# Pairs of weight blocks in the split products of w_in: four products with the high parts, then two with the low parts

## The chip, the cores and the metric

The kernel runs on one core of one Trainium2 chip. The metric is the device time of one execution in microseconds (us). The engines go by the names of the profile: PE is TensorE (its matrix products), PEld its loads of weights, DVE is VectorE, ACT is ScalarE, POOL is GpSimd, and SP is the queue that issues most DMAs.

## The reference

One layer over 512 latent and 128 context tokens (640 in all), all in float32, cut here to what comes before, in and behind the changed products:

```python
D_MODEL = 2048
P_IN = C_SHIFT + 2 * D_B          # 3360 + 2048 columns

def _layer(x, mod, s0, shift_fn, lp):
    sh1, sc1, g1, sh2, sc2, g2 = jnp.split(mod, 6, axis=-1)
    h = _rmsnorm(x, lp['norm1_g']) * (1.0 + sc1) + sh1
    p = h @ lp['w_in']
    o_a, s_fin = _rwkv7_bidir(shift_fn(p[..., :C_SHIFT], lp['mu_shift']), s0, lp)
    o_b = _chunk_gmlp(jax.nn.gelu(p[..., C_SHIFT:]), lp)
    x = x + g1 * (jnp.concatenate([o_a, o_b], axis=-1) @ lp['w_out'])
    h = _rmsnorm(x, lp['norm2_g']) * (1.0 + sc2) + sh2
    ff = (jax.nn.silu(h @ lp['w_ffn_gate']) * (h @ lp['w_ffn_up'])) @ lp['w_ffn_down']
    return x + g2 * ff, s_fin
```

The change is in `p = h @ lp['w_in']` alone. `_rwkv7_bidir` is a two-way recurrence over 16 heads, which the kernel works off in chunks of 64 tokens; `_chunk_gmlp` mixes tokens within chunks of 128.

## The kernel before

**Stages.** The w_in stage (with the modulation and the normalisation ahead of it), the recurrence together with w_out, and the feed-forward part. They share PE, one after the other.

**The w_in stage.** `h` lies transposed in SBUF, 16 blocks of 128 rows by 640 tokens, split into two float32r tiles: `h_hi` and `h_lo`, the rest that the rounding left. `w_in` comes in 43 column blocks of 128, each in four pieces of 512 rows (256 KB). `split` loads a piece (L167, issued from SP), casts it to `hi` on ACT (L168) and takes the rest `lo` on DVE (L169), with three buffers for each of the three tiles; `prefetch` runs two pieces ahead. `win` works off one piece: for each half of the tokens (320 columns) and each of its four blocks it issues three products of 128x128 weights by 320 columns, hi by h_hi (L190), hi by h_lo (L191) and lo by h_hi (L192). They add up in one PSUM tile `big` per half over the four pieces of a block, 48 products in all; the last one closes the sum. Over the stage there are 4128 of these wide products.

**What lies between them.** When a block is done, `take` copies it to SBUF (`praw`, ACT L959) and hands it to a generator that works it off in small steps: the token shift, per pair of heads (eight pairs, two directions each) the key normalisation (products `pmm`, L519), decay and gate (`pwa`, L592 and L593, read by ACT as sg and tha, L596), the Gram matrices of the chunks (`pG`, L651, copied as GB, L655 and L663), transposes (`pXT`, L669, copied as XT, L675, and stored to DRAM, L677) and a product `pW` (L683, copied as Z, L685), and for the gMLP blocks a gelu (`gq`, L706 to L713). `pmm`, `pwa`, `pG`, `pXT` and `pW` share two PSUM tiles, so each waits until its forerunner there has been copied out; XT has two SBUF buffers. A second generator, `solve`, takes the Gram blocks through DRAM (`mix<-dd`, by POOL's queue) and inverts them on DVE (from L802 on); a third, `merge`, fetches the result (`TB<-d`, POOL's queue) and puts it together by five small products per direction (`pblk` L843, `pM` L868 copied as `M` L871, `pT` L877 copied as TF, L880). Beside these, four more columns of modulation weights are loaded (1 MB each, L893) and multiplied (`pm`, L906).

**What sets the order.** Behind the second and the fourth block of a half (`GRAN`), `between` lets each of the three queues of generators run for a budget of estimated costs. The generators thus hand their instructions out at fixed places of the program; but outside the first part of the stage and the recurrence, the order on each engine is that of the scheduler, which works through the program by its dependences. Each engine takes its instructions strictly in that order.

## Time and profile before

| | us |
|---|---|
| median of 3 timed runs | 3223.48 (3221.9 to 3225.47) |
| the profiled execution | 3213.3 |
| its span, first to last instruction | 3211.5 |
| mean granted clock of PE | 0.991 |
| first and last start of L190 | 49.4 and 1078.8 |

A row of a group of instructions reads: line, engine, operation, tile written <- tiles read, shapes, count, then busy time and the mean ns of one, then the idle time of the engine just before them and what ended it. Products overlap in PE's pipeline, so 0.31 us of busy time each does not say how far apart they start; the timeline's start column does. An idle time in brackets is one in which no product was under way. The line numbers in the profile are those of the kernel before.

### The profile page before, as it was taken

Reading aid. Unit: us, or ns where it says so; the run is one execution under the profiler, and the core shown is the slowest. Engines: PE = TensorE matmul, PEld = TensorE weight load, DVE = VectorE, ACT = ScalarE, POOL = GpSimd, SP = SyncE. Lnnn points to the kernel's source line nnn. Section 1 sums busy time; section 2 is a strip of 40 time slices with the busy share of each in tenths; the row PEclk is TensorE's granted clock in tenths of the full one; section 3 lists DMA queues with packets and bytes.
Section 4 is the critical chain, followed back from the end, with each engine's and each line's share of the span. In section 5 each row is a group of like instructions: output and inputs, shape, how many; then the busy total and the mean of one; then the engine's idle time right before and its main releaser. Section 6 shows DMA issues by size and latency. Waiting matters only on the chain.

```text
span 3211.5 us, 72260 instructions
## 1 busy us (share of the span) xinstructions
PE 3088.0 (96%) x28216; PEld 2858.2 (89%) x28216; DVE 2330.3 (73%) x4107; ACT 1460.1 (45%) x3197; POOL 1219.0 (38%) x1065
## 2 busy tenths in 40 slices
PE   6999989999999999999999999999999999999997
PEld 3688778788878888899999999999999999999997
DVE  4558666676657677767877777777777788887788
ACT  3344544454444444346644444444444454444365
POOL 2001121211122024311465566556655645555542
PEclk9999999999999999999999999999999999999999
DMA  9767786777778687564434434343344364553453
GB/s 372 239 187 203 210 215 171 209 218 193 201 198 216 210 275 253 173 200 133 141 116 130 127 105 123 118 124 118 113 128 126 104 199 152 159 165 112 140 165 122
DMA packets 740438, 550.88 MB, mean 172 GB/s; under 512 B 141056, under 2 KB 673504, under 8 KB 731264
## 3 DMA queue, kind: packets, MB, share of 16 engines
q1 hardware_dynamic: 727136, 532.47, 55.0%
q0 software_dynamic: 10624, 13.23, 1.9%
q8 instruction: 222, 3.64, 0.5%
q14 instruction: 120, 0.98, 0.1%
q10 hardware_dynamic: 2336, 0.57, 0.1%
HBM read 437.79 MB, written 110.95 MB: 171 GB/s over the span
## 4 chain that ended last, share of the span: by engine, by line
PE 56%; DVE 5%; issue 4%; DMA 3%; POOL 2%; ACT 2%; SPq 0%; DVEq 0%; POOLq 0%; ACTq 0%
PE P L1644 15%; PE P L1642 15%; PE P L1643 15%; DVE lo L1424 1%; PE big L1482 1%; PE big L1484 1%; PE big L1483 1%; PE big L1039 1%; PE big L190 1%; PE big L192 1%; PE big L191 1%; PE big L1041 1%; PE big L1040 1%; DMA opd<-d_op 1%; DMA rawd<-in_w_ffn_down_dram 1%
## 5 line engine op out<-in xcount | busy, mean ns | idle before, releaser
L1644 PE MATMUL P<-xo,lo 128*128 128x320 f32 x2352 | 727.1, 309 | 0.8 <-DVE lo L1424 0.7
L1642 PE MATMUL P<-xo,hi 128*128 128x320 f32 x2352 | 727.0, 309 | 0.7 <-ACT hi L1423 0.7
L1643 PE MATMUL P<-xo,hi 128*128 128x320 f32 x2352 | 726.9, 309 | 0.0
L1424 DVE TENSOR_TENSOR lo<-raw,hi 128x512 fp32r<-128x512 f32 x526 | 500.8, 955 | 174.4 <-ACT hi L1423 169.9
L1423 ACT CAST hi<-raw 128x512 fp32r<-128x512 f32 x526 | 326.7, 621 | 484.0 <-PE P L1643 392.1
L190 PE MATMUL big<-h_hi,hi 128*128 128x320 f32 x1376 | 447.3, 325 | 8.1 <-ACT hi L168 4.5
L1644 PEld LDWEIGHTS P<-xo,lo 128*128 128x128 f32 x2352 | 441.5, 188 | 1.8 <-DVE lo L1424 1.8
L1642 PEld LDWEIGHTS P<-xo,hi 128*128 128x128 f32 x2352 | 441.6, 188 | 1.0 <-ACT hi L1423 1.0
L1643 PEld LDWEIGHTS P<-xo,hi 128*128 128x128 f32 x2352 | 441.6, 188 | 0.0
L192 PE MATMUL big<-h_hi,lo 128*128 128x320 f32 x1376 | 431.1, 314 | 0.7 <-DVE lo L169 0.6
L191 PE MATMUL big<-h_lo,hi 128*128 128x320 f32 x1376 | 431.1, 313 | 0.7 <-DVE h_lo L352 0.4
L1552 POOL TENSOR_TENSOR raw<-raw 128x512 f32<-128x512 f32 x252 | 408.5, 1631 | 14.1 <-DVE lo L1424 2.7
L1644 PE MATMUL P<-xd,lo 128*128 128x320 f32 x1232 | 384.5, 312 | 16.3 <-DVE lo L1424 16.2
L1642 PE MATMUL P<-xd,hi 128*128 128x320 f32 x1232 | 382.7, 311 | 1.5 <-ACT hi L1423 0.3
L1643 PE MATMUL P<-xd,hi 128*128 128x320 f32 x1232 | 381.4, 310 | 0.0
L169 DVE TENSOR_TENSOR lo<-raw,hi 128x512 fp32r<-128x512 f32 x268 | 183.4, 689 | 200.6 <-ACT hi L168 185.1
L190 PEld LDWEIGHTS big<-h_hi,hi 128*128 128x128 f32 x1376 | 260.9, 190 | 58.1 <-issue 34.8
L1423 ACT CAST hi<-rawd 128x512 fp32r<-128x512 f32 (+1 forms) x288 | 168.8, 587 | 240.7 <-PE P L1643 203.1
L168 ACT CAST hi<-raw 128x512 fp32r<-128x512 f32 x268 | 164.5, 618 | 225.7 <-PE big L191 123.8
L191 PEld LDWEIGHTS big<-h_lo,hi 128*128 128x128 f32 x1376 | 261.3, 190 | 5.1 <-DVE h_lo L352 1.1
L192 PEld LDWEIGHTS big<-h_hi,lo 128*128 128x128 f32 x1376 | 260.3, 189 | 5.6 <-DVE lo L169 1.6
L1644 PEld LDWEIGHTS P<-xd,lo 128*128 128x128 f32 x1232 | 231.9, 188 | 23.2 <-DVE lo L1424 22.8
(404 smaller groups left out, 6052.8 us busy)
## 6 DMA issues: line engine op xcount, KB each, us to landing
wt<-in_w_mod_dram SPq DMA_DIRECT2D x96, 1024.0 KB
raw<-in_w_ffn_gate_dram SPq DMA_DIRECT2D x182, 256.0 KB
raw<-in_w_ffn_up_dram SPq DMA_DIRECT2D x182, 256.0 KB
rec<-d_S SPq DMA_DIRECT2D x80, 576.0 KB
raw<-in_w_in_dram SPq DMA_DIRECT2D x172, 256.0 KB
rawd<-in_w_ffn_down_dram SPq DMA_DIRECT2D x128, 256.0 KB
raw<-in_w_out_dram SPq DMA_DIRECT2D x96, 256.0 KB
xd<-d_os SPq DMA_DIRECT2D x66, 320.0 KB
```

What stands on the lines that cost most here:

```text
L168: S.copy(hi, raw)
L169: V.tensor_sub(lo, raw, hi.bitcast(F32))
L190: TE.matmul(halves[hf], hi[:, k, :], h_hi[:, kb, s], start=(kb == 0), stop=False)
L191: TE.matmul(halves[hf], hi[:, k, :], h_lo[:, kb, s], start=False, stop=False)
L192: TE.matmul(halves[hf], lo[:, k, :], h_hi[:, kb, s], start=False, stop=(kb == KB - 1))
L1039: TE.matmul(halves[hf], hi[:, k, :], o_hi[kb][:, s], start=(k == 0), stop=False)
L1423: S.copy(hi[:, 0:nk], raw[:, 0:nk])
L1424: V.tensor_sub(lo[:, 0:nk], raw[:, 0:nk], hi[:, 0:nk].bitcast(F32))
L1552: G.tensor_tensor(out=o[:, 0:nk], in0=p[:, 0:nk], in1=q[:, 0:nk], op=ALU.subtract)
L1642: TE.matmul(ps, hi[:, k, :], xk[:, 0, :], start=f, stop=False)
L1643: TE.matmul(ps, hi[:, k, :], xk[:, 1, :], start=False, stop=False)
L1644: TE.matmul(ps, lo[:, k, :], xk[:, 0, :], start=False, stop=l)
```

## The change

The core of the diff:

```diff
@@ -189,7 +189,9 @@
                 kb = 4 * q + k
                 TE.matmul(halves[hf], hi[:, k, :], h_hi[:, kb, s], start=(kb == 0), stop=False)
                 TE.matmul(halves[hf], hi[:, k, :], h_lo[:, kb, s], start=False, stop=False)
-                TE.matmul(halves[hf], lo[:, k, :], h_hi[:, kb, s], start=False, stop=(kb == KB - 1))
+                if k % 2:
+                    for j in (kb - 1, kb):
+                        TE.matmul(halves[hf], lo[:, j - 4 * q, :], h_hi[:, j, s], start=False, stop=(j == KB - 1))
                 wide[0] += 1
                 step(k)
```

The two lo products of blocks 0 and 1, and those of blocks 2 and 3, now stand together behind the four hi products of the same blocks. Number, shapes and operands of the products stay; the sum in PSUM gets its terms in another order. `step(k)` hands out small work at k = 1 and 3 only, so it still comes behind a whole pair. From L192 on, the changed kernel's line numbers are two higher (its lo products are L194).

The scheduler answers with another order of the small work on PE, ACT, DVE and SP between wide products 384 and 3974 of the stage, mostly by a few places. The first of the two places that matter is on PE, in the fifth pair of heads. Before, the merge of the fourth pair begins behind wide product 2328 (`pblk`):

```order
L192 MATMUL big<-h_hi,lo 128x320
L843 MATMUL pblk<-TB,A__1119 32x32 x2
L725 MATMUL pw<-ident,wsp 128x128
L843 MATMUL pblk<-TB,A__1119 32x32
L651 MATMUL pG<-R,X 128x128 x4
L190 MATMUL big<-h_hi,hi 128x320
```

and behind wide product 2376, with the transposes `pXT` 25 to 33 wide products back, comes

```order
L192 MATMUL big<-h_hi,lo 128x320
L906 MATMUL pm_6577<-wt,cT 2x512 x8
L843 MATMUL pblk<-TB,A__1119 32x32 x14
L683 MATMUL pW_7173<-Z,GA 64x64 x10
L843 MATMUL pblk<-TB,A__1119 32x32 x23
L592 MATMUL pwa<-wa,wh 128x320
```

Now nothing small stands behind product 2328; the merge begins behind 2352, and behind 2376 stands

```order
L194 MATMUL big<-h_hi,lo 128x320 x2
L908 MATMUL pm_6577<-wt,cT 2x512 x2
L671 MATMUL pXT<-ident,X 128x64 x16
L908 MATMUL pm_6577<-wt,cT 2x512 x2
L845 MATMUL pblk<-TB,A__1119 32x32 x4
L671 MATMUL pXT<-ident,X 128x64 x4
L908 MATMUL pm_6577<-wt,cT 2x512 x4
L685 MATMUL pW_7173<-Z,GA 64x64 x10
L594 MATMUL pwa<-wa,wh 128x320
```

The first part of the merge moved 24 wide products back, and the transposes (L669, now L671) moved behind product 2376, directly ahead of `pW` (L683, now L685).

The second place is on ACT, in the third pair of heads, where the second pair's `M` is copied. Before:

```order
L675 COPY XT<-pXT 128x128 x2
L685 COPY Z<-pW_4747 64x5x64 x2
L685 COPY Z<-pW_4748 64x5x64 x2
L711 ACTIVATE gq<-gq 128x640
L959 COPY praw<-big 128x320
L871 COPY M_5109<-pM_5143 32x320 x2
```

Now:

```order
L677 COPY XT<-pXT 128x128
L687 COPY Z<-pW_4747 64x5x64 x2
L677 COPY XT<-pXT 128x128
L713 ACTIVATE gq<-gq 128x640
L961 COPY praw<-big 128x320
L687 COPY Z<-pW_4748 64x5x64 x2
L873 COPY M_5109<-pM_5143 32x320 x2
```

The last two copies of Z moved behind the tanh of the gelu (L711, now L713). On PE the second `pmm` product (L519), which writes to the tile that these copies read, stands behind wide product 1720 now (1715 before), and `pT` behind 1728 as before. On DVE, in the same place, the gelu's product `gq` (L709) and the wait of `solve` for its DMA (L802) stood so before:

```order
L755 TENSOR_TENSOR vt_4929<-vt_4929,lng 128x640
L802 COPY mx_1121<-mix 80x2x15
L169 TENSOR_TENSOR lo<-raw,hi 128x512
L806 TENSOR_TENSOR mix<-mx_1121,mix 80x2x28
L756 TENSOR_TENSOR vt_4929<-vt_4929,lnb 128x640
L808 TENSOR_TENSOR mx_1121<-mx_1121,mix 80x2x14x2
L709 TENSOR_TENSOR gq<-gq,praw 128x640
```

and stand so now:

```order
L169 TENSOR_TENSOR lo<-raw,hi 128x512
L757 TENSOR_TENSOR vt_4929<-vt_4929,lng 128x640
L804 COPY mx_1121<-mix 80x2x15
L711 TENSOR_TENSOR gq<-gq,praw 128x640
L808 TENSOR_TENSOR mix<-mx_1121,mix 80x2x28
```

`gq` (now L711) comes directly behind L802 (now L804) instead of four instructions later.

## The prediction

> **What bounds the kernel now.** I read the page first, then the windows by stage, then the timeline of TensorE inside the w_in stage, then its waits. The page:

> ```profile
> span 3211.5 us, 72260 instructions
> PE 3088.0 (96%) x28216; PEld 2858.2 (89%) x28216; DVE 2330.3 (73%) x4107; ACT 1460.1 (45%) x3197; POOL 1219.0 (38%) x1065
> L190 PE MATMUL big<-h_hi,hi 128*128 128x320 f32 x1376 | 447.3, 325 | 8.1 <-ACT hi L168 4.5
> L192 PE MATMUL big<-h_hi,lo 128*128 128x320 f32 x1376 | 431.1, 314 | 0.7 <-DVE lo L169 0.6
> ```

> PE is busy 96% of the span and nearly nothing ends late before the three lines that the change reorders: 0.7 us of idle time before all 1376 products of L192. These lines run from 49 to 1079 us. The windows of that stage and of what follows (columns: length, then each engine's busy time and instructions, then the granted clock, DMA share and GB/s):

> ```profile
> 160.00:420.00 260.00, 254.68 (x2403) 216.66 (x2402) 171.81 (x331) 116.80 (x245) 36.80 (x61) 1.00 0.73 203
> 420.00:660.00 240.00, 225.47 (x2768) 186.43 (x2768) 154.00 (x310) 112.57 (x250) 43.33 (x73) 0.98 0.73 199
> 660.00:1080.00 420.00, 404.12 (x5474) 346.62 (x5474) 284.91 (x577) 200.28 (x429) 79.66 (x125) 1.00 0.72 197
> ```

> So PE is the stage's bound. Its open idle time is 5.3 + 14.5 + 15.9 = 35.7 us (length less busy); that is all a better order could take away. The order of the engines' instructions differs only up to the first instructions of the next stage, so I cost the w_in stage alone.

> **The products themselves: 0.** The same 4128 products are issued; what changes is which follows which. A piece of the timeline shows the pace and the price of an interruption by small products (start, busy, engine, line):

> ```profile
> 1070.10 0.31 PE L190 MATMUL big<-h_hi,hi 128*128 128x320 f32 x1
> 1070.24 0.31 PE L191 MATMUL big<-h_lo,hi 128*128 128x320 f32 x1
> 1070.39 0.31 PE L192 MATMUL big<-h_hi,lo 128*128 128x320 f32 x1
> 1070.54 0.31 PE L190 MATMUL big<-h_hi,hi 128*128 128x320 f32 x1
> 1070.68 0.31 PE L191 MATMUL big<-h_lo,hi 128*128 128x320 f32 x1
> 1070.83 0.31 PE L192 MATMUL big<-h_hi,lo 128*128 128x320 f32 x1
> 1071.07 0.82 PE L868 MATMUL pM<-TB,GB 32*32 32x32 f32 x40
> 1071.82 0.41 PE L190 MATMUL big<-h_hi,hi 128*128 128x320 f32 x1
> 1072.07 0.31 PE L191 MATMUL big<-h_lo,hi 128*128 128x320 f32 x1
> ```

> From 1070.10 to 1070.83 five steps take 0.73 us, 146 ns each. L190 to L191 keeps the weights and changes the moving tile; L191 to L192 changes both; L192 to L190 changes the weights and keeps h_hi's tile. All cost the same. The new order has only steps of these kinds (two lo products in a row change weights and moving columns), so it neither gains nor loses at the pace. The page's means (325 against 314) are not a price of the first product: they hold the longer one behind an interruption.

> **Fewer interruptions: -1.2 us.** Leaving the wide run costs 1071.07 - 1070.83 - 0.15 = 0.09 us, coming back 1072.07 - 1071.82 - 0.15 = 0.10: about 0.2 us for a round trip. Counted along PE's order there are 305 such trips before and 299 after: 6 x 0.2 = -1.2 us (bounds -1.2 and 0, if the small products then stand in worse places).

> **The later low part: -0.6 us.** A lo tile is now needed behind four products of its piece rather than two, 2 x 0.146 = 0.29 us later. What waits for it (us, times, before the load of weights of L192):

> ```profile
>   DVE lo L169: 2.2, 4
> ```

> Four waits can each lose at most 0.29 us: -1.2 us; they may go to another wait behind them: 0. I take the middle. No DMA and no queue is moved past by this itself: hi is needed as early as before, the last product of a block is still a lo product, so the copy of its result (L959) starts as before, and the hi buffer is free one product sooner for a cast (L168) that PE hardly waits for (4.5 us above).

> **The rearranged small work.** This is where time can come and go. PE's waits in the stage (total, times, longest):

> ```profile
> PE pT L877 <- ACT M L871: 4.6, 4, 3.4
> PE pW L683 <- ACT XT L675: 3.8, 4, 1.7
> PE pwa L592 <- ACT Z L685: 2.3, 3, 1.0
> ```

> Two places carry most of the difference; the order rows stand in the part on the change. The first is the merge of the fourth pair and the transposes of the fifth. Before, pblk (L843) came 24 wide products sooner than it now does and waited for its DMA:

> ```profile
> 630.48 0.22 PE L843 MATMUL pblk<-TB,A__1119 32*32 32x32 f32 x2 [1.24 <-DMA TB<-d]
> 631.51 0.22 PE L843 MATMUL pblk<-TB,A__1119 32*32 32x32 f32 x2 [0.55 <-DMA TB<-d]
> 645.32 0.42 PE L592 MATMUL pwa<-wa,wh 128*128 128x320 f32 x1 [0.42 <-ACT Z L685]
> ```

> 24 x 0.146 = 3.5 us covers that: -1.8 us. In exchange the transposes pXT (L669), which had 33 wide products between them and pW (L683), stand directly ahead of it with only ten small ones of L906 and L843. That is a figure that the kernel already has in two other places, of which the dearer reads:

> ```profile
> 427.12 0.27 PE L669 MATMUL pXT<-ident,X 64*128 64x64 f32 x1 [0.65 <-ACT XT L675]
> 427.61 0.34 PE L669 MATMUL pXT<-ident,X 64*128 64x64 f32 x3 [0.22 <-ACT XT L675]
> 427.88 1.04 PE L906 MATMUL pm<-wt,cT 128*2 128x512 f32 x8
> 430.60 0.80 PE L683 MATMUL pW<-Z,GA 64*64 64x64 f32 x20 [1.69 <-ACT XT L675]
> 432.35 0.43 PE L592 MATMUL pwa<-wa,wh 128*128 128x320 f32 x1 [0.95 <-ACT Z L685]
> 641.81 0.27 ACT L675 COPY XT<-pXT 128x128 f32<-128x128 f32 x1 [5.15 <-DMA d_S<-XT]
> ```

> Its idle times add to 3.5 us, 0.42 of which the place has already: +3.1 (no more than 0 if the copies come at once; 5.15 + 0.95 - 0.42 = 5.7 if the third copy again waits 5.15 us for the store of the first, last row, with nothing over it). Together with the -1.8: **+1.3 us**, bounds -1.8 and +3.9.

> A long idle has a second price. Behind the 3.4 us wait for M the clock was granted at less, and the wide products came slower:

> ```profile
> 476.00:478.00 2.00, 1.80 (x44) 1.71 (x43) 1.90 (x7) 1.92 (x5) 0.00 (x0) 0.75 0.72 201
> 478.00:482.00 4.00, 4.00 (x95) 3.65 (x95) 3.66 (x13) 1.75 (x5) 1.01 (x1) 0.70 0.93 290
> 477.96 0.47 PE L190 MATMUL big<-h_hi,hi 128*128 128x320 f32 x1
> 478.23 0.47 PE L191 MATMUL big<-h_lo,hi 128*128 128x320 f32 x1
> ```

> Half rate for 0.25 x 2 / 0.5 + 0.30 x 4 / 0.5 = 3.4 us, with 270 ns a product for 146: 3.4 x (1 - 146/270) = 1.6 us lost. Whether the new idle does the same is open: 0 to +1.6, I take **+0.7**. [...]

> The second place is ACT's copy of M for the second pair's merge (start, busy, line, idle before and its releaser):

> ```profile
> 467.84 0.85 ACT L685 COPY Z<-pW 64x320 f32<-64x320 f32 x2 [0.37 <-PE pW L683]
> 474.27 0.74 ACT L711 ACTIVATE gq<-gq 128x640 f32<-128x640 f32 x1 [5.58 <-DVE gq L709]
> 474.91 0.41 ACT L959 COPY praw<-big 128x320 f32<-128x320 f32 x1
> 475.34 0.86 ACT L871 COPY M<-pM 32x320 f32<-32x320 f32 x2
> 475.81 0.24 PE L877 MATMUL pT<-TF,M 32*32 32x32 f32 x2 [3.41 <-ACT M L871]
> 471.69 0.19 DVE L802 COPY mx<-mix 80x30 f32<-80x30 f32 x1 [2.75 <-DMA mix<-dd]
> 473.42 0.82 DVE L709 TENSOR_TENSOR gq<-gq,praw 128x640 f32<-128x640 f32 x1
> ```

> DVE's L802 stands waiting for a DMA and holds L709, this holds ACT's L711, and this the M copy that PE waits for. In the new order L709 follows L802 directly: it starts at 471.9 instead of 473.4, so L711 is done at 471.9 + 0.82 + 0.74 = 473.4. But the last two Z copies (L685, from the third pair) now stand behind L711 and L959: they are done at 473.4 + 0.4 + 0.9 = 474.7. The second pmm product (L519), which needs their bank, therefore holds PE eight wide products ahead of pT until 474.7; with 8 x 0.146 + 0.3 us more pT starts at 476.2 instead of 475.8: **+0.4 us**. Bounds: -1.5 (pT gets L709's gain in full) and +2 (the DMA that L802 waits for is issued later by the work that is now ahead of it).

> The other transposes: eight pairs in two directions make sixteen of them; over the nine others whose distance to pW differs, the wide products between sum to 16 fewer, 16 x 0.146 = 2.3 us if every one were uncovered, 0 if none is; before, pW waited 3.8 us in four places: **+0.7**.

> Sum: 0 - 1.2 - 0.6 + 1.3 + 0.7 + 0.4 + 0.7 = **+1.3 us**. The profiled execution took 3213.3 us (span 3211.5 and 1.8 around it), so 3214.6 for such a one; it lies 10 us under the median of the timed runs, 3223.5, and I forecast for these **3225 us**.

> **The rivals.** *Slower.* The place of the pXT row of 641.81: ACT's third copy waits for the store of the first, and nothing lies over it. Then that place costs +3.9, the half clock +1.6, the same lack of cover in the other pairs +2.3 and the DMA behind L802 +2: with -1.8 from the first two terms +8.0, **3231.5 us**. It decides from the point where the transposes stand under about 5 us ahead of pW. For it: the order rows show that cover gone at one pair for certain; against it: two of the sixteen have the same figure before and cost 3.5 us at most.

> *Faster.* The new order happens to relieve the waits: M -4.6 (all four), TB -1.8, lo -1.2, trips -1.2: -8.8, **3214.7 us**. For it: 35.7 us lie idle in the stage, and DVE now puts lo behind small work that others wait for. Against it: of PE's merge products most stand at the same wide product as before, and the 3.4 us wait has only moved.

> *Weights.* If a product with weights that are in place were cheaper, four hi products in a row would gain. The timeline rows exclude it, and the old order had the same pairs.

> **How the numbers follow.** About the same (the sum within 6.4 us, which is 0.2%, about what a measurement of this kernel can tell from no change): 0.52. Slower: 0.30, since the one certain change of cover goes that way. Faster: 0.18. The bounds of the terms add to -1.2 - 1.2 - 1.8 - 1.5 = -5.7 and 3.9 + 1.6 + 2 + 2.3 = +9.8, hence 3217.8 to 3233.3; the many small shifts that I did not cost one by one, and the rivals' ends, widen it to 3214 to 3237.

> **What would show it.** Right: wide products 146 ns apart in any order; a wait for XT ahead of pW near wide product 2376 (about 650 us) and none for TB there; PE held at pmm instead of pT near 471 to 476 us; the stages behind 1080 us equally long. Wrong: a pace other than 146 ns between two lo products, or PE's idle time in 160 to 1080 us far from 36 us.

## The result, and the profile after

| | before | changed |
|---|---|---|
| median, 10 runs each (us) | 3224.19 (3221.9 to 3227.8) | 3214.89 (3211.87 to 3220.58) |
| ratio | | 0.9966, interval 0.9957 to 0.9976 |
| the profiled execution (us) | 3213.3 | 3213.29 |
| its span, its mean granted clock | 3211.5, 0.991 | 3211.5, 0.992 |

By the timed runs the changed kernel is 9.3 us faster, where no change was forecast; the time itself lies at the lower end of the stated range. (The ratio and its interval are taken from the runs themselves and need not be the quotient of the medians. Two runs of the sessions below, one of before and one of `lopair`, took 14122 and 5894 us; the ratios leave them out.) By the two profiled executions nothing happened at all. The page after (span, engines, two of the three product lines) reads:

```profile
span 3211.5 us, 72254 instructions
PE 3090.4 (96%) x28216; PEld 2861.2 (89%) x28216; DVE 2337.4 (73%) x4107; ACT 1461.6 (46%) x3197; POOL 1213.9 (38%) x1065
L190 PE MATMUL big<-h_hi,hi 128*128 128x320 f32 x1376 | 437.9, 325 | 5.1 <-ACT h_hi L353 2.9
L194 PE MATMUL big<-h_hi,lo 128*128 128x320 f32 x1376 | 324.4, 313 | 0.3 <-DVE lo L169 0.3
```

The same number of products, as long as before on average (325 and 313 ns; before 325 and 314). L194's smaller busy sum (324.4 us for 431.1) is only overlap: two of its products follow each other (0.45 us of busy time for both, 0.31 for one alone), and the sum counts the time in which both are under way once. The windows of the stage (length, busy time and instructions of each engine, granted clock, DMA share, GB/s):

```profile
160.00:420.00 260.00, 253.86 (x2480) 216.82 (x2478) 170.19 (x331) 116.80 (x247) 36.87 (x61) 1.00 0.72 202
420.00:660.00 240.00, 228.35 (x2713) 188.47 (x2714) 158.66 (x320) 113.81 (x250) 43.27 (x73) 0.97 0.74 201
660.00:1080.00 420.00, 405.14 (x5454) 346.29 (x5454) 284.09 (x572) 203.31 (x432) 79.11 (x125) 1.00 0.71 197
```

PE's open idle time is now 6.1 + 11.7 + 14.9 = 32.7 us; it was 35.7. Three microseconds: 2.8 less in the middle window, where both places of the prediction lie, 1.0 less in the third and 0.8 more in the first.

Of the second place, the timeline of the changed kernel (POOL's issue of the DMA that `solve` waits for, DVE's first copy behind it and the gelu product, four rows of ACT, PE's wait), and from before the one issue that the prediction didn't show:

```profile
461.64 0.54 POOL L798 DMA_DIRECT2D mix<-dd  x1 [3.14 <-DMA dd<-GB]
466.38 0.19 DVE L804 COPY mx<-mix 80x30 f32<-80x30 f32 x1 [0.78 <-DMA mix<-dd]
466.47 0.81 DVE L711 TENSOR_TENSOR gq<-gq,praw 128x640 f32<-128x640 f32 x1
467.31 0.74 ACT L713 ACTIVATE gq<-gq 128x640 f32<-128x640 f32 x1 [1.99 <-DVE gq L711]
467.96 0.41 ACT L961 COPY praw<-big 128x320 f32<-128x320 f32 x1
468.38 0.85 ACT L687 COPY Z<-pW 64x320 f32<-64x320 f32 x2
469.25 0.86 ACT L873 COPY M<-pM 32x320 f32<-32x320 f32 x2
469.28 0.81 PE L521 MATMUL pmm<-fs,bones 128*128 128x320 f32 x2 [0.99 <-ACT Z L687]
```

```profile
465.18 0.54 POOL L796 DMA_DIRECT2D mix<-dd  x1 [3.73 <-DMA dd<-GB]
```

The chain is the one foretold: L804, L711, L713, `praw`, Z, `pmm`. But L804 begins at 466.4 us; before, L802 began at 471.7, and the prediction kept that time (2.4 us of the difference had built up before this place). PE idles 0.99 us for `pmm` and not at all for `pT` behind it; before, `pT` waited 3.41 us. The windows of the changed kernel behind that wait keep the full clock (the last but two columns: 1.00, against 0.75 and 0.70 before):

```profile
471.00:475.00 4.00, 4.00 (x136) 3.54 (x135) 3.65 (x13) 2.61 (x6) 1.01 (x1) 1.00 1.08 305
475.00:479.00 4.00, 4.00 (x64) 3.77 (x64) 3.90 (x13) 1.78 (x6) 0.00 (x0) 1.00 0.98 317
```

Of the first place, the timeline of PE in the changed kernel (the wait for TB is gone, the one for XT is there):

```profile
634.35 0.71 PE L671 MATMUL pXT<-ident,X 64*128 64x64 f32 x16
636.14 0.42 PE L671 MATMUL pXT<-ident,X 64*128 64x64 f32 x4
...
638.73 0.80 PE L685 MATMUL pW<-Z,GA 64*64 64x64 f32 x20 [1.20 <-ACT XT L677]
640.48 0.41 PE L594 MATMUL pwa<-wa,wh 128*128 128x320 f32 x1 [0.95 <-ACT Z L687]
```

1.20 + 0.95 = 2.15 us of idle, where the prediction took over 3.5 from another pair of heads.

### The profile page after: what moved, and what is told of

The parts are those of the page before. It is cut to its first block, busy times and chain, and to the rows that moved or that the text cites. A ratio compares the mean times of both kernels' runs of the same rounds, so it can differ in the third digit from the quotient of the medians.

```text
span 3211.5 us, 72254 instructions
## 1 busy us (share of the span) xinstructions
PE 3090.4 (96%) x28216; PEld 2861.2 (89%) x28216; DVE 2337.4 (73%) x4107; ACT 1461.6 (46%) x3197; POOL 1213.9 (38%) x1065
## 4 chain that ended last, share of the span: by engine, by line
PE 56%; DVE 6%; issue 4%; DMA 3%; POOL 2%; ACT 2%; SPq 0%; DVEq 0%; POOLq 0%; ACTq 0%
PE P L1646 15%; PE P L1644 15%; PE P L1645 15%; DVE lo L1426 1%; PE big L1486 1%; PE big L1485 1%; PE big L1484 1%; PE big L190 1%; PE big L1041 1%; PE big L194 1%; PE big L191 1%; DMA rawd<-in_w_ffn_down_dram 1%; DMA opd<-d_op 1%; PE big L1043 1%; PE big L1042 1%
## 5 line engine op out<-in xcount | busy, mean ns | idle before, releaser
L190 PE MATMUL big<-h_hi,hi 128*128 128x320 f32 x1376 | 437.9, 325 | 5.1 <-ACT h_hi L353 2.9
L191 PE MATMUL big<-h_lo,hi 128*128 128x320 f32 x1376 | 423.0, 314 | 0.9 <-DVE h_lo L354 0.9
L169 DVE TENSOR_TENSOR lo<-raw,hi 128x512 fp32r<-128x512 f32 x268 | 184.3, 692 | 199.3 <-ACT hi L168 197.9
L194 PE MATMUL big<-h_hi,lo 128*128 128x320 f32 x1376 | 324.4, 313 | 0.3 <-DVE lo L169 0.3
L190 PEld LDWEIGHTS big<-h_hi,hi 128*128 128x128 f32 x1376 | 261.5, 190 | 52.0 <-issue 31.1
L168 ACT CAST hi<-raw 128x512 fp32r<-128x512 f32 x268 | 164.5, 617 | 234.3 <-PE big L191 115.2
L191 PEld LDWEIGHTS big<-h_lo,hi 128*128 128x128 f32 x1376 | 261.1, 190 | 6.2 <-DVE h_lo L354 1.9
L1646 PEld LDWEIGHTS P<-xd,lo 128*128 128x128 f32 x1232 | 231.7, 188 | 22.8 <-DVE lo L1426 22.5
L1426 DVE TENSOR_TENSOR lo<-rawd,hi 128x512 fp32r<-128x512 f32 (+1 forms) x288 | 228.0, 797 | 28.2 <-ACT hi L1425 24.9
```

The source lines that it names most:

```text
L168: S.copy(hi, raw)
L169: V.tensor_sub(lo, raw, hi.bitcast(F32))
L190: TE.matmul(halves[hf], hi[:, k, :], h_hi[:, kb, s], start=(kb == 0), stop=False)
L191: TE.matmul(halves[hf], hi[:, k, :], h_lo[:, kb, s], start=False, stop=False)
L194: TE.matmul(halves[hf], lo[:, j - 4 * q, :], h_hi[:, j, s], start=False, stop=(j == KB - 1))
L1426: V.tensor_sub(lo[:, 0:nk], raw[:, 0:nk], hi[:, 0:nk].bitcast(F32))
```

## The experiments

All were timed in four sessions on three chips; the kernels of a session share its runs of before. `quad` has 6 runs and `quadffn` 8, the others 11 or 12, before 29 to 35. The letters in the expectations: W (later O) says that the gain is how the small work falls among the wide products; P, that pairs make the products themselves cheaper; H, that it lies in the first three blocks; E, elsewhere; C, that only the granted clock differs; A, that the prediction's second place carries the gain; B, that it needs the other places too.

| session | kernel | median (us) | before (us) | ratio (interval) | difference to before at equal clock (us) |
|---|---|---|---|---|---|
| 1 | aa | 3224.05 | 3222.44 | 1.0014 (1.0004 to 1.0023) | +2.3 |
| 1 | again | 3218.98 | | 0.9991 (0.9982 to 1.0) | -1.5 |
| 1 | head | 3223.84 | | 1.0011 (0.9999 to 1.0023) | +2.7 |
| 1 | main | 3218.11 | | 0.9988 (0.9979 to 0.9998) | -2.7 |
| 2 | lofirst | 3224.95 | 3222.39 | 1.0009 (0.9995 to 1.0023) | -0.7 |
| 2 | lopair | 3230.48 | | 1.0017 (1.0008 to 1.0027) | +0.4 |
| 2 | quad | 3211.28 | | 0.9963 (0.9948 to 0.9977) | -9.7 |
| 2 | ffn | 3220.41 | | 0.9994 (0.9981 to 1.0006) | -1.9 |
| 3 | first | 3217.63 | 3223.17 | 0.9979 (0.9968 to 0.9991) | -2.9 |
| 3 | second | 3222.36 | | 1.0 (0.999 to 1.001) | +0.9 |
| 3 | one | 3217.5 | | 0.9983 (0.9973 to 0.9992) | -2.5 |
| 3 | quadffn | 3207.67 | | 0.9953 (0.9936 to 0.9969) | -11.9 |
| 4 | only | 3221.61 | 3226.03 | 0.9985 (0.9973 to 0.9996) | -3.7 |
| 4 | allbut | 3224.11 | | 0.9996 (0.9986 to 1.0007) | -1.1 |
| 4 | again2 | 3218.08 | | 0.9981 (0.9971 to 0.9992) | -5.0 |

The last column is an estimate. Each timed run has its time and its mean granted clock on record; a straight line through all runs of a session, with one slope for the session (1.8 to 2.3 us for each 0.001 of clock) and a constant for each kernel, gives what is left between a kernel and before when their clocks are equal. Its error is about 1 us, and `aa`, the same instructions as before, shows that 2 us can come of nothing.

One profile of each gives the time of a stretch of wide products, from the start of the first to that of the last, numbered along PE's order. In brackets is how much of the stretch ran at half clock, granted 0.50 (us). The first four kernels have before's order of PE's small work, the next four the changed kernel's, apart from two `pm` products that stand behind product 288 or behind 384 (in `head` and `main` as the edit has it there).

| products | before, aa, ffn, head | after, again, main, again2 | only | allbut | first | second | one | quad |
|---|---|---|---|---|---|---|---|---|
| 288 to 1248 | 196.8, 197.1, 197.0, 197.3 | 196.8, 196.4, 196.4, 196.4 | 196.7 | 196.8 | 196.4 | 196.3 | 197.3 | 196.3 |
| 1248 to 1488 | 68.9, 68.0, 69.3, 67.7 | 67.3, 70.2 (3), 68.1, 69.9 (3) | 68.1 | 68.3 | 66.8 | 68.5 | 65.8 | 65.9 |
| 1632 to 1776 | 46.7 (3), 44.8, 46.5 (7), 46.5 (7) | 43.1, 43.7, 43.3, 43.9 | 43.1 | 46.5 (3) | 43.3 | 45.5 (3) | 43.4 | 44.2 |
| 2112 to 2304 | 58.4 (3), 57.5, 59.5 (3), 59.8 (3) | 59.9 (3), 59.6 (3), 59.8 (3), 59.9 (3) | 61.0 (7) | 62.3 (7) | 60.4 (7) | 59.8 (3) | 59.5 (3) | 59.7 (3) |
| 2304 to 2400 | 26.4, 28.1 (3), 26.8, 26.1 | 26.0, 25.9, 26.1, 27.1 (3) | 27.5 (3) | 25.9 | 26.2 | 28.4 (3) | 28.2 (3) | 27.8 (3) |
| 2496 to 2592 | 24.3, 24.7, 27.1 (3), 27.3 (3) | 23.1, 23.1, 23.2, 23.7 | 26.0 (3) | 22.8 | 21.1 | 23.9 | 22.5 | 22.8 |
| 2784 to 2928 | 49.6, 49.8, 49.8, 50.1 | 52.5, 51.7, 51.5, 51.0 | 49.7 | 51.9 | 49.6 | 51.7 | 54.3 (3) | 48.7 |
| 288 to 4127 | 940.8 (10), 941.9 (20), 947.6 (24), 947.3 (34) | 940.7 (17), 942.2 (14), 941.9 (20), 942.0 (24) | 945.3 (31) | 950.6 (31) | 940.2 (24) | 947.2 (31) | 944.6 (27) | 934.9 (20) |

**Session 1: is it real, and is it in the first blocks?** `aa` is before unchanged, `again` the changed kernel. `head` has pairs in the first three column blocks alone, `main` (`wide[0] >= 96`) in the other forty:

```diff
-                TE.matmul(halves[hf], lo[:, k, :], h_hi[:, kb, s], start=False, stop=(kb == KB - 1))
+                if wide[0] < 96:
+                    if k % 2:
+                        for j in (kb - 1, kb):
+                            TE.matmul(halves[hf], lo[:, j - 4 * q, :], h_hi[:, j, s], start=False, stop=(j == KB - 1))
+                else:
+                    TE.matmul(halves[hf], lo[:, k, :], h_hi[:, kb, s], start=False, stop=(kb == KB - 1))
```

> The kernel before, unchanged, for its own noise, its clocks and a second profile. Theory W (waits): its w_in stage holds more or longer waits of TensorE and more stretches at half clock than the changed kernel's; the one profiled execution of before (3213.3 us, against 3221.9 to 3227.8 for ten timed runs) was an unusually short one. Then the spans here are near 3222 us, and a second profile shows the stage's last wide product some 5 to 10 us later than 1079.3 us. Theory E (elsewhere): the w_in stage ends at 1079 us as in the first profile and the timed runs lose their 10 us somewhere else. Both expect a ratio of 1.000 within 0.001.

> The changed kernel again, beside the unchanged one on the same chip. Both theories: ratio 0.995 to 0.998. Theory W: a second profile with the last wide product at about 1077 us, and PE idle in 160 to 1080 us of about 33 us.

> Pairs only in the first three blocks of w_in (288 of 4128 wide products, up to about 135 us); the later small work stays where it was. Theory P (the products themselves run faster in pairs) expects 288/4128 of 9 us: -0.7 us, ratio 0.9998. Theory W expects the gain to come from rearranged small work behind 135 us, so nothing here: 1.000 within 0.001. A third, H (the gain lies in the first 135 us, by lo waits there and the stretches at half clock behind them; the two profiles differ by 2.3 us at wide product 287), expects -2 to -6 us: 0.998 to 0.9995.

> Pairs in the other forty blocks alone (3840 of 4128 wide products), with the small work in the changed kernel's order. Theory W and theory P: -7 to -9 us, ratio 0.997 to 0.998. Theory H: -3 to -7 us less than the whole change, ratio 0.998 to 1.000.

`aa` and before, the same instructions, differ by 0.14%, so no ratio here is surer than that. Against `aa` the changed kernel gains 5.1 us and `main` 5.9, `head` 0.2. H falls. The gain is real, and on this chip nearer to 5 us than to 9. `again` and `main`, expected at ratios of 0.995 to 0.998 and 0.997 to 0.998 by W, came out at 0.9991 and 0.9988. E falls too: from the start of product 4127 to the end, before, `aa` and `head` take 2132 to 2137 us, the changed kernel, `again` and `main` 2134 to 2137. But W's picture of before was off as well: the stage of `aa` ended at 1081.5 us, 2 us later than in the first profile and not 5 to 10.

**Session 2: pairs, or the order of the small work?** `lofirst` keeps triples with the low part first; `lopair` makes pairs of them, two low products and then four high ones. The scheduler gives both the same order of the small work on every engine, a third one with 294 interruptions. `quad` takes eight high products, then four low ones. `ffn` leaves w_in as it was and makes pairs in the feed-forward part. The changed lines, of `lopair`, `quad` and `ffn` in turn:

```diff
+                if k % 2:
+                    for j in (k - 1, k):
+                        TE.matmul(halves[hf], lo[:, j, :], h_hi[:, 4 * q + j, s], start=(4 * q + j == 0), stop=False)
+                    for j in (k - 1, k):
+                        TE.matmul(halves[hf], hi[:, j, :], h_hi[:, 4 * q + j, s], start=False, stop=False)
+                        TE.matmul(halves[hf], hi[:, j, :], h_lo[:, 4 * q + j, s], start=False, stop=(4 * q + j == KB - 1))
...
+                if k == 3:
+                    for j in range(4):
+                        TE.matmul(halves[hf], lo[:, j, :], h_hi[:, 4 * q + j, s], start=False, stop=(4 * q + j == KB - 1))
...
+                    if k % 2 or k == nk - 1:
+                        for j in range(k - k % 2, k + 1):
+                            TE.matmul(ps, lo[:, j, :], x(i, 4 * q + j)[:, 0, :], start=False, stop=l and j == k)
```

> Triples as before, but the low part first: lo by h_hi, hi by h_hi, hi by h_lo. The scheduler answers with a third order of the small work (294 interruptions; before 305, with pairs 299). Theory O (the gain is an accident of how the small work falls among the wide products; pairs as such do nothing): the time is that of this order, somewhere within 10 us of before (3222), and the same as that of lopair within 2 us. Theory P (four hi products ahead of two lo products make the wide products themselves cheaper): no gain from triples, 3222 to 3225 us. Theory C (the difference is only how long PE's clock happens to be granted at half rate): time follows the granted clock, some 1.9 us for each 0.001, whatever the order.

> Pairs with the low parts first: two lo products, then four hi products. The order of the small work on every engine, and the wide product behind which each piece stands, is that of lofirst to the last instruction; only the wide products within six differ. Theory O: the same as lofirst within 2 us. Theory P: 5 us faster than lofirst, as the changed kernel is than before. Theory C: as its clock is, 1.9 us for each 0.001, with wide products 146 ns apart.

> Eight products with the high parts of four blocks, then the four low ones. The scheduler gives a fourth order of the small work (298 interruptions). Theory O: its own value within 10 us of before, in either direction, not foretold by the number of hi products in a row. Theory P: at least what the pairs gain, 3217 us or less. Theory C: as its clock is.

> Pairs in the feed-forward part alone (3584 blocks of three products of 320 columns), the w_in stage as before with its small work in the same order. Theory O: no change in w_in; in the feed-forward part nothing from the pace, at most some us from the waits for lo (17 to 19 us there now, each lo product now needed two products later or sooner): 3218 to 3224 us. Theory P: 5 x 3584 / 1376 = 13 us faster, 3209 us. Theory C: as its clock is.

P falls twice. `lopair` is no faster than `lofirst` (ratios 1.0017 and 1.0009, intervals overlapping, where P wanted 5 us less), and pairs in all 3584 blocks of the feed-forward part bring 2 us by the medians and 6 at most by the interval, where P wanted 13. The timeline of the changed kernel and that of `lopair` show why (x2 is two low products in one row):

```profile
1068.01 0.45 PE L194 MATMUL big<-h_hi,lo 128*128 128x320 f32 x2
1068.30 0.31 PE L190 MATMUL big<-h_hi,hi 128*128 128x320 f32 x1
1068.45 0.31 PE L191 MATMUL big<-h_lo,hi 128*128 128x320 f32 x1
1068.60 0.31 PE L190 MATMUL big<-h_hi,hi 128*128 128x320 f32 x1
1068.74 0.31 PE L191 MATMUL big<-h_lo,hi 128*128 128x320 f32 x1
1068.89 0.45 PE L194 MATMUL big<-h_hi,lo 128*128 128x320 f32 x2
```

```profile
1081.76 0.45 PE L192 MATMUL big<-h_hi,lo 128*128 128x320 f32 x2
1082.05 0.31 PE L194 MATMUL big<-h_hi,hi 128*128 128x320 f32 x1
...
1082.63 0.45 PE L192 MATMUL big<-h_hi,lo 128*128 128x320 f32 x2
```

Six products take 0.88 and 0.87 us, 146 ns each. From low product to low product the median of the steps at full clock is 146 ns in the changed kernel (some 650 of them); of all steps between wide products it is 147, before and after. `lopair` and `quad`, both with more than one low product in a row and fewer interruptions than before, come out at 3230 and 3211 us: neither the grouping nor the number of interruptions alone tells which way it goes. `lofirst` and `lopair` don't test the interruptions cleanly: they need lo first, and their products wait 8.4 and 10.3 us for it (before: 0.6). O missed too: it wanted these two within 2 us, and the medians are 5.5 us apart. The clock is the second effect: the profile of `lopair` had 34 us of half clock in 288 to 4127, that of `lofirst` 24, at the same order of the small work, and at equal clock both kernels lie within 1 us of before.

**Session 3: which places?** `first` has pairs up to wide product 2016 and triples behind it, `second` the reverse (the condition `wide[0] < 672` in the diff of `head`, and its opposite). `one` is a mixture within a pair, hi0 hi0 hi1 lo0 hi1 lo1:

```diff
                 TE.matmul(halves[hf], hi[:, k, :], h_hi[:, kb, s], start=(kb == 0), stop=False)
+                if k % 2:
+                    TE.matmul(halves[hf], lo[:, k - 1, :], h_hi[:, kb - 1, s], start=False, stop=False)
                 TE.matmul(halves[hf], hi[:, k, :], h_lo[:, kb, s], start=False, stop=False)
-                TE.matmul(halves[hf], lo[:, k, :], h_hi[:, kb, s], start=False, stop=(kb == KB - 1))
+                if k % 2:
+                    TE.matmul(halves[hf], lo[:, k, :], h_hi[:, kb, s], start=False, stop=(kb == KB - 1))
```

`quadffn` is `quad` with the edit of `ffn`.

> Pairs up to wide product 2016, triples behind it. The order of the small work is the changed kernel's up to product 2016 and nearly so up to 2376, both places of the prediction included, and that of before from 2498 on. Theory O (each place costs what its own order of small work costs, wherever the pairs are): products 1632 to 1776 take 43 to 44 us as in the changed kernel (before: 45 to 47), 2304 to 2400 26 us without the wait for TB, 2784 to 2928 50 us as before (changed kernel: 52); the stage 940 to 943 us less the scatter of the clock, the whole 2 to 5 us under before. Theory P (pairs as such pay): half of the products in pairs, half of the gain, 2 to 3 us. Theory C (only the clock): same places as before.

> Triples up to wide product 2016, pairs behind it. The order of the small work is that of before up to product 2016 and at 2304 to 2400, so both places of the prediction are undone although the second stands among pairs; from 2466 on it is the changed kernel's. Theory O: products 1632 to 1776 45 to 47 us as before, 2304 to 2400 26 to 28 us with the wait for TB, 2496 to 2592 23 us as in the changed kernel (before: 24 to 27), 2784 to 2928 52 us; the whole within 3 us of before. Theory P: half of the gain. Theory C: as the clock is.

> A third order within a pair: hi0 hi0 hi1 lo0 hi1 lo1, so the loads of weights alternate more than in either kernel. The order of the small work is that of before up to product 1274 and at 2304 to 2400, and the changed kernel's at 1274 to 1720. Theory O: products 1632 to 1776 43 to 44 us without the wait for M, 2304 to 2400 as before with the wait for TB; the whole 1 to 4 us under before. Theory P: loads alternate, no pairs: no gain, 3222 us or more. Wide products 146 ns apart within the six in any theory but one in which alternating weights cost.

> Eight high products, then four low ones in w_in (as in quad, the same order of the small work), and pairs in the feed-forward part. Theory O: w_in as in quad, so 9 to 11 us under before for the whole, again with fewer or shorter waits in products 1248 to 1488 and 2784 to 2928; 0 to 2 us more from the feed-forward part. Theory C: quad's gain does not come back.

`first` and `one` gain 5.5 and 5.7 us, `second` nothing. What `first` and `one` share with the changed kernel, and `second` does not, is the order at products 1274 to 1720: the second place and what leads up to it. `one` has it without a single pair of low products, and its order at the first place, TB's wait included, is that of before. Of the expectations on stretches nearly all came true (1632 to 1776: 43.3, 43.4 and 45.5 us); the wholes of `first` and `one` gained somewhat more than the 2 to 5 and 1 to 4 us expected. `quadffn` has quad's gain again and is, at 3207.67 us, the fastest kernel of the study: 15.5 us under before, more than the 9 to 13 expected.

**Session 4: the place alone.** `only` has pairs in wide products 1272 to 1776 (`424 <= wide[0] < 592`) and there alone the changed kernel's order; `allbut` is the complement. `again2` issues the changed kernel's instructions in its order.

> Pairs in wide products 1272 to 1776 alone. The order of the small work is the changed kernel's at products 1274 to 1720 and that of before everywhere else. If the second place of the prediction carries the gain (theory A): products 1632 to 1776 take 43 to 44 us (before: 45 to 47), every other stretch as before, the whole 3 to 5 us under before, as first and one. If the gain needs the other places too (theory B): within 2 us of before, even if that stretch is shorter.

> Pairs everywhere in w_in but in wide products 1272 to 1776. The order of the small work is that of before at products 1274 to 1720 and the changed kernel's everywhere else. Theory A: products 1632 to 1776 take 45 to 47 us with the wait for M; 2112 to 2304 1 us longer than before, 2304 to 2400 1 us shorter, 2496 to 2592 2 to 3 us shorter, 2784 to 2928 2 us longer; the sum and the whole within 2 us of before. Theory B: 2 to 4 us faster.

> The changed kernel's instructions once more, in the same order, beside only and allbut. Both theories: 3 to 6 us faster than before; theory A: as only within 2 us; theory B: faster than only and allbut, about by the sum of both.

The ratios add up: -0.15% for `only`, -0.04% for `allbut`, -0.19% for the whole. By the ratios and at equal clock (3.7 of 5.0 us) the place alone carries about three quarters, by the medians a little over half, 4.4 of 8.0 us; the complement cannot be told from nothing. `only` and `allbut` came out as theory A has it. `again2` did not by its median: it gained 8.0 us, 3.5 more than `only`, where A wanted 2 at most and B about the sum of both. With intervals of 0.1% to either side, and 0.14% between identical kernels, the whole times favour A and don't settle it. The profiled spans of `only` and `allbut` (3223.9 and 3225.2 us) don't show it, since both had 31 us of half clock in the stage; the stretches of the table do (1632 to 1776: 43.1 and 46.5 us). The timelines of `only`, then of `allbut`, show the chain switched over (POOL's issue, DVE's copy behind the DMA, PE's wait):

```profile
463.58 0.54 POOL L800 DMA_DIRECT2D mix<-dd  x1 [2.82 <-DMA dd<-GB]
468.35 0.19 DVE L806 COPY mx<-mix 80x30 f32<-80x30 f32 x1 [0.81 <-DMA mix<-dd]
471.26 0.81 PE L523 MATMUL pmm<-fs,bones 128*128 128x320 f32 x2 [0.82 <-ACT Z L689]
```

```profile
464.87 0.54 POOL L800 DMA_DIRECT2D mix<-dd  x1 [3.75 <-DMA dd<-GB]
471.33 0.19 DVE L806 COPY mx<-mix 80x30 f32<-80x30 f32 x1 [2.72 <-DMA mix<-dd]
475.46 0.24 PE L881 MATMUL pT<-TF,M 32*32 32x32 f32 x2 [3.38 <-ACT M L875]
```

Wide product 1632 starts at 442.8 and 442.9 us. In `only` the DMA is issued 1.3 us sooner and takes 4.8 us to the copy behind it instead of 6.5: 3.0 us sooner in all, and PE waits 0.82 us instead of 3.38.

*Is it the clock alone (C)?* No, by the last column of the table: at equal clock `only` and `again2` still gain 3.7 and 5.0 us, `quad` 9.7 and `quadffn` 11.9. But the clock is part of most differences here, and by this estimate all of what made `lopair` slow.

## Why the prediction was wrong

The step that failed, before all others, is the second place, "+0.4 us. Bounds: -1.5 ... and +2". It followed DVE's wait, the gelu, ACT's queue and PE correctly, but let the whole chain begin where it began before, at the landing of `mix<-dd`; its bound allowed that the DMA comes later, not that it comes sooner. Measured from the start of wide product 1632, the DMA was issued after 21.0 us instead of 22.1 and DVE was released after 25.7 instead of 28.6: 1.1 us by the issue and 1.8 by a quicker transfer. Before's own profile is the extreme one of its order. The six profiles with the order of before here (the four, `second` and `allbut`) have the issue after 21.8 to 22.6 us and DVE's copy after 27.1 to 28.6, the seven with the changed order (the four, `only`, `first` and `one`) after 20.7 to 21.1 and 25.4 to 26.1.

What else had moved is SP's queue of loads, which the prediction did not look at. The issues of `w_in` pieces around this place and the window from 17 to 21 us behind product 1632 (the last but one column is the DMA engines' busy share), before and then in the changed kernel:

```profile
459.31 0.71 SPq L167 DMA_DIRECT2D raw<-in_w_in_dram  x1
463.46 0.68 SPq L167 DMA_DIRECT2D raw<-in_w_in_dram  x1
460.06:464.06 4.00, 4.00 (x101) 3.15 (x105) 3.06 (x9) 2.94 (x6) 1.39 (x3) 1.00 0.81 187
```

```profile
453.90 0.97 SPq L167 DMA_DIRECT2D raw<-in_w_in_dram  x2
471.94 2.38 SPq L167 DMA_DIRECT2D raw<-in_w_in_dram  x3
457.67:461.67 4.00, 4.00 (x29) 2.37 (x32) 3.01 (x9) 3.30 (x7) 0.86 (x3) 1.00 0.44 97
```

Before, two pieces are issued 16.2 and 20.4 us behind product 1632, while `dd<-GB` and `mix<-dd` are under way; in the changed kernel the last piece ahead of them goes out after 13.8 us and the next after 31. In that window the DMA engines' busy share is 0.77 to 1.01 in the six profiles and 0.40 to 0.50 in the seven; the last `dd<-GB`, issued at nearly the same point (17.2 to 18.0 and 17.3 to 17.5 us), lands after 21.1 to 21.9 and 20.1 to 20.4 us. That the loads held the transfers up fits all thirteen profiles; no run moves the loads alone.

The two waits (Z for `pmm`, M for `pT`) then shrink together: over 1632 to 1776 the four kernels of each order average 46.1 and 43.5 us, **-2.6 for the +0.4** of the forecast. Only some 1.1 us of it is idle time of PE, which falls from 3.2 to 2.1 us on average. The larger part is the clock: five of the six profiles with the order of before show a half-clock stretch behind the wait, of the seven with the changed order none. The four of before average 4.3 us of it, 2.0 us lost at the prediction's own price of 1.6 us for 3.4 us.

The terms one by one, by the means of the two groups of four (the row for the low part by the two profiles alone):

| term of the sum | forecast (us) | measured (us) |
|---|---|---|
| products | 0 | 0: 147 ns a step before and after |
| fewer interruptions | -1.2 | not separable |
| later low part | -0.6 | -1.4: PE waits 0.8 us for lo instead of 2.2 |
| first place, 2304 to 2400 | +1.3, clock +0.7 | 26.9 to 26.3: -0.6 |
| second place, 1632 to 1776 | +0.4 | 46.1 to 43.5: -2.6 |
| other covers of the transposes | +0.7 | 25.9 to 23.3 (2496 to 2592): -2.6; 49.8 to 51.7 (2784 to 2928): +1.9; 58.8 to 59.8 (2112 to 2304): +1.0 |

The row for the low part, in the changed kernel's view of L194 (loads of weights and products, as the prediction's row for L192):

```profile
  DVE lo L169: 0.8, 2
```

That is past the forecast's bound of -1.2. Both rows count one moment twice, at the load and at its product (76.1 us before, 75.2 now), and all but one of these waits lie ahead of product 288.

*First place.* The mechanism held: TB's wait went, XT's came. The size was off: 2.15 us of idle where 3.5 were taken from another pair of heads, so that with the clock term -0.6 stands for +2.0, a miss nearly as large as that of the second place. The clock term came to nothing: in this stretch one of the four profiles of either order has a half-clock stretch. (Over all kernels, such a stretch comes with the wait for TB in four of seven profiles, with the wait for XT in one of the six that have the changed kernel's order here and in both `quad` and `quadffn`.)

*Other covers.* The prediction counted only transposes here. What moved most were other waits. PE's timeline before (first row), and after (second and third):

```profile
696.50 0.82 PE L868 MATMUL pM<-TB,GB 32*32 32x32 f32 x40 [1.66 <-DVE TF L860]
```

```profile
690.21 0.82 PE L870 MATMUL pM<-TB,GB 32*32 32x32 f32 x40
...
790.73 0.81 PE L521 MATMUL pmm<-fs,bones 128*128 128x320 f32 x2 [2.10 <-ACT Z L687]
```

A wait of 1.66 us for DVE's TF went away (all four of before's order have it, one of the other four, with 1.11), and with it most of the -2.6. The wait of 2.10 for Z (0.55 to 2.10 in the four) does not explain the +1.9 of 2784 to 2928: other waits went there, and PE's idle time in that stretch fell, from 2.4 to 3.0 us to 1.1 to 2.7. What lengthened it was not followed.

*The rivals.* "Faster" had the right mechanism, waits relieved by the new order, and, at 3214.7, nearly the time measured; it had a chance of 0.18. That its number fits is luck: in the two profiles the waits for M fell by 3.3 us and not 4.6, new waits of `pmm` for Z came to 3.6, and later comparisons gave less than 9 us. The argument against it, that "the 3.4 us wait has only moved", fell in part: a wait of 0.99 us moved to `pmm`, the rest was gone. "Weights" was rightly excluded. "Slower" named waits that came (XT, Z), each smaller than what went.

*The base.* The sum was made against a profiled execution that was itself lucky: 10 us of half clock between products 288 and 4127, where three others of the same order had 20, 24 and 34. Over the whole execution it had 57 us, those three 68 to 86, the changed kernel's profile 55. So the two profiled spans agree while the medians do not.

*What stays open.* The means of the eight profiles account for 2.7 us between products 288 and 4127 (944.4 to 941.7). The comparisons say 9.3, 3.5 (5.1 against `aa`) and 8 us. Some 2 us more show ahead of product 288, where the changed kernel, `again` and `again2` take 85.4 to 85.7 us and before, `aa`, `ffn`, `only` and `main` 87.2 to 89.0; but `first`, `allbut` and `head`, with the same products in pairs there, take 86.2, 87.2 and 89.4, so the pairs alone do not explain it. Half clock goes with it: up to product 288 the changed kernel, `again`, `again2` and `first` have 10 to 15 us of it, before, `aa`, `ffn`, `only`, `main` and `allbut` 17 to 19, `head` 25. The first comparison came out largest in part by the clock: the changed kernel's ten runs had 0.9907 on average, `again` and `again2` 0.9894, which is worth 2.5 us at 1.9 us for each 0.001. The rest is within what identical kernels showed (0.14%, 4.5 us). Why `lopair` spends more time at half clock than `lofirst` isn't settled.

## What to carry to other kernels

When an edit makes a scheduler rearrange work, each wait has to be followed back to the issue of the DMA behind it, and that issue, and the loads that other queues issue beside it, have to be placed in the new order too; a landing time from the old trace is no fixed point (here DVE was released 25.7 us behind product 1632 instead of 28.6). Orders of the same products in one stage lie 19 us apart here (`quad` 3211, `lopair` 3230; about 10 at equal clock) at an unchanged pace (147 and 146 ns a product in the timelines of the two), so trying a few inner orders and keeping the fastest is worth more than arguing for one of them. For effects of a few microseconds, compare stretches between two counted instructions over several profiles: apart from the half-clock stretches in them most repeat to within 1 us, while a single span of the same order moves by 12 (3211.5 to 3223.5). And compare at equal granted clock.

## What the runs showed of the hardware

At the same place of the program the granted clock dropped from 1.00 to 0.50 in some executions and not in others. Behind wide product 3624 all kernels but `quad`, `quadffn`, `lofirst` and `lopair` have the same small products in the same order. These are windows of `aa`, then of before, ahead of that place and at it, cut at the same distance from the product:

```profile
956.10:959.51 3.41, 2.33 (x32) 1.16 (x28) 0.00 (x0) 2.76 (x8) 3.41 (x7) 1.00 0.37 63
959.51:969.75 10.24, 8.49 (x63) 6.36 (x56) 2.73 (x5) 5.18 (x12) 0.80 (x2) 0.50 1.00 259
```

```profile
955.39:958.80 3.41, 2.33 (x32) 1.15 (x28) 0.00 (x0) 2.76 (x8) 3.41 (x7) 1.00 0.35 58
958.80:969.04 10.24, 7.86 (x81) 6.20 (x74) 3.94 (x7) 6.19 (x15) 0.79 (x2) 1.00 1.00 269
```

The same 1.08 us of idle PE time (3.41 - 2.33) is followed by 10.2 us at half clock in one execution and by none in the other; other kernels had 3.4 and 6.8 there. Products 3600 to 3660 take 21.1 to 21.3 us without a stretch and up to 23.9 with the longest.

Whole runs follow the granted clock too: a line through 90 timed runs (those of session 1 with their before, and the changed kernel's first ten), with a constant for each kernel, falls by 1.9 us for each 0.001 of mean clock.
